# Scoring the two heads of a pair in the two row halves of TensorE, in a two-block transformer kernel

## The chip, the cores and the metric

One core of one Trainium2 chip runs the whole program. The metric is device time in microseconds (us), from the start of a launch to its end. The inputs are fp32, and the output is compared with the reference in fp32.

## The reference

Two transformer blocks on 512 tokens of width 1024. The first holds the change: its mixer is sparse attention of two kinds, and a mixture of 32 experts follows. The second block (differential attention and retention) is not touched.

```python
z = h @ w_in                                  # split into q, k, v of all branches
qn = rms_norm(q heads)                        # 8 NSA heads in 2 groups, 8 MoBA heads, 64 wide
kc = rms_norm(_compress(k_cmp)); vc = _compress(v_cmp)     # 31 compressed keys per group
s = qn . kc * scale - slope * distance;  p_cmp = masked_softmax(s);  o_cmp = p_cmp . vc
# selected branch and window branch: with 512 tokens both are causal attention over all keys
o_nsa = g0 * o_cmp + g1 * softmax(q . k_slc) . v_slc + g2 * softmax(q . k_win) . v_win
o_moba = softmax(q . k) . v                   # causal too at this length
x1 = x + gate * (concat(o_nsa, o_moba) @ w_out);  then the experts, then the second block
```

The scores need fp32 accuracy, so each factor is split into a high and a low part (fp32r, one pass of the array each), and products of parts are added in PSUM.

## The kernel before

The program is one list of instructions per engine, in the order in which Python generators yield. `first_half` computes the projections z in chunks (`zchunk`): a step is three matmuls of 512 columns (lines 257 to 259). `weave` runs such a main generator and, at a rate per step, one step of a background generator: compression (`compress`), the stacks of q (`q_stacks`), compressed scores (`compressed`), then `nsa`, which makes the stacks of k and calls `heads`.

`heads` works on 12 jobs. Jobs 0 to 7 are NSA (4 pairs of heads, 2 branches each), jobs 8 to 11 MoBA (4 pairs). A job is two heads, `hh` 0 and 1, and four tiles of 128 queries, `i` 3 to 0, against 512, 384, 256 and 128 keys (never under 256 columns on TensorE). In 8 rounds x, list A does the scores of the new job and list B the work of the job before: `turn` transposes the probabilities (line 917, copied out at 921 by ScalarE or VectorE), `pv` multiplies them by v (line 936, two heads in the two column halves of the array, 128*64). Each entry of A and B ends in a yield. A score tile is `scores` (lines 875 and 876), then on VectorE bias and maximum (line 881), on ScalarE the exponential (line 883). `normal` divides two tiles by their sum: reciprocal and gate on VectorE (894, 896), the products on GpSimd for head 0 (902) and on VectorE for head 1 (904).

To score a head of width 64 with all 128 rows, q is stacked: its high part lies in the head's own 64 rows, its low part in the other 64; k's high part stands twice, and so does its low part. Two passes then give all four products. `stacks` builds this from a transposed pair (`pair_turn`): a scaling to SBUF (334), copies (341, 343, 350) and subtractions (348, 351, 353), some of them moving data to the other half of the partitions. For MoBA this is done per job, in `prep`, while the job before is scored.

When the projections end, jobs 5 to 11 go on alone: `middle` loads `ada_w` in `mods` (lines 638 and 641, four column quarters), and takes 9 background steps between two of its loads, then drains the rest, and the output product follows (from 328.84 us). PSUM has a ring of three banks for scores and transposes while the projections run, and of six after. In the experts, line 1580 adds a bias by matmuls of 64 rows, in pairs: one in the upper and one in the lower half of the array's rows.

```python
    mm(ps[:, :w], lhsT=q, rhs=b.k[hh][0][:, :w], start=True, stop=False)     # 875
    mm(ps[:, :w], lhsT=q, rhs=b.k[hh][1][:, :w], start=False, stop=True)     # 876
```

Of the kernel before, what the change touches and what calls it, by code (L numbers as in the profile page):

```python
# [9 lines left out]
F32R = mybir.dt.float32r  # L10
# [4 lines left out]
OP = mybir.AluOpType  # L15
# [4 lines left out]
P = 128  # L20
# [167 lines left out]
class Build:  # L188
# [139 lines left out]
    def stacks(self, rows, c, gain, q=None, k=None, slow=False):  # L328
# [6 lines left out]
        if slow:  # L335
            yield
# [19 lines left out]
        yield  # L356

# [296 lines left out]
    def compress(self):  # L654
# [19 lines left out]

        self.kcb = ar.get(F32R)
# [74 lines left out]
        k0, k1 = kc[:, 0, :, 96:128], kc[:, 1, :, 96:128]  # L750
        nc.scalar.mul(k0, p2, gk)
        nc.vector.scalar_tensor_tensor(k1, p2, gk, k0, op0=OP.mult, op1=OP.subtract)
# [3 lines left out]
    def q_stacks(self):  # L756

        ar = self.ar
        self.qs = [ar.get(F32R), ar.get(F32R)]
        fb = ar.get()  # L760
        for c in range(4):
            self.f = fb.cols(c * T, T)
            yield from self.stacks(lambda i: self.qn.cols(i * T, T), c, self.gq[:, 0, c:c + 1],
                                   q=[self.qs[c // 2].cols((2 * (c % 2) + hh) * T, T) for hh in range(2)])
        ar.put(fb)
        ar.put(self.qn)

    def compressed(self):
# [10 lines left out]
        for g in range(2):  # L779
            ps = self.sb()  # L780
            for p in range(2):
                for j in range(4):
                    h = 4 * g + j
                    mm(ps, lhsT=self.kc[:, p, g, 96 - 32 * j:224 - 32 * j], rhs=self.qs[h // 4].cols((h % 4) * T, T),
                       start=(p == 0 and j == 0), stop=(p == 1 and j == 3))
# [75 lines left out]
    def heads(self, jobs):  # L861
# [6 lines left out]
        def scores(b, hh, i):  # L868
            n = (i + 1) * P
            w = max(n, 256)  # L870
            h = 2 * b.c + hh
            sl = 2.0 ** -(h % 8 + 1)
            ps = self.sb()
            q = b.q[hh][:, i * P:(i + 1) * P]
            mm(ps[:, :w], lhsT=q, rhs=b.k[hh][0][:, :w], start=True, stop=False)
            mm(ps[:, :w], lhsT=q, rhs=b.k[hh][1][:, :w], start=False, stop=True)
# [13 lines left out]
        def normal(b, hh, lo):  # L890
# [6 lines left out]
            for i in (lo + 1, lo):  # L897
# [49 lines left out]
        after = []  # L947
# [5 lines left out]
        for s in range(n + 1):  # L953
# [3 lines left out]
            if new:  # L957
                for hh in range(2):
                    for i in (3, 2, 1, 0):
                        A.append([lambda hh=hh, i=i: scores(new, hh, i)])  # L960
                        if i in (2, 0):
                            after.append(lambda new=new, hh=hh, i=i: normal(new, hh, i))
                            A[-1].append(len(after))
# [6 lines left out]
            for x in range(max(len(A), len(B))):  # L970
                if x < len(A):
                    A[x][0]()
                    yield
# [4 lines left out]
                if x % 2 == 0 and (x or old) and (A or not x):  # L978
                    after.pop(0)()
# [5 lines left out]
    def nsa(self):  # L985
# [4 lines left out]
        for c in range(4):  # L990
            for br in range(2):
# [4 lines left out]
                b.q = [self.qs[g].cols(((2 * c + hh) % 4) * T, T) for hh in range(2)]  # L996
                b.k = [self.kst[br, g]] * 2
# [8 lines left out]
    def moba(self):  # L1006
# [3 lines left out]
        for c in range(4):  # L1010
# [4 lines left out]
            def prep(b=b, c=c):  # L1015
                if c == 0:
                    self.flush()
                    mo.extend(ar.get(F32R) for _ in range(3))
# [3 lines left out]
                b.q = [mo[0].cols((2 * (c % 2) + hh) * T, T) for hh in range(2)]  # L1022
                b.k = [[mo[1 + c % 2].cols((2 * hh + x) * T, T) for x in range(2)] for hh in range(2)]
                self.f = self.cm.cols(512, T)
# [11 lines left out]
    def first_half(self):  # L1036
# [29 lines left out]
        self.bg = [self.compress(), self.q_stacks(), cmp]  # L1066
# [1365 lines left out]
```

## Time and profile before

| | |
|---|---|
| three runs | 1747.45, 1748.62, 1750.28 us (median 1748.62) |
| profiled execution | 1749.42 us, its span 1747.7 us |
| first scores of job 0, end of the projections | 139.35 us, 232.87 us |
| first scores of jobs 8, 9, 10, 11 | 267.7, 280.93, 294.87, 308.62 us |
| output product begins | 328.84 us |

A span is from the first to the last instruction; the 1.7 us around it are launch and end. A row of a timeline gives the start, the modelled length, the engine, the line and the operation, with output and inputs by name; 128*64 means that 128 rows and 64 columns of the array are used, 128x512 that 512 columns stream. Modelled ends of matmuls overlap the next start, so what a matmul costs is read from one start to the next. Releasers in brackets say who ended the idle time before.

### The profile page before, as it was taken

To read this page: it belongs to the slowest core of one execution; us is meant where nothing else is said; L and a number is where in the kernel's file an instruction comes from. 1 tells how busy PE (TensorE), PEld (TensorE's weight loads), DVE (VectorE), ACT (ScalarE), POOL (GpSimd) and SP (SyncE) were. 2 spreads that over 40 slices of the span, in tenths; PEclk is the share of its full clock that TensorE was granted. 3 is DMA by queue.
4 is the path that set the end of the run, shared out by engine and by line. 5 is a ranking of instruction groups with operands and counts; after the bars stand their busy time and mean duration, and the time that the engine had idled before them with its cause. 6 is when DMAs were issued, how large, how long until landed. Compare 5 with 4: busy or idle time off the path is not lost. (4 is left out here: it accounts for less than half of the span.)

```text
span 1747.7 us, 21964 instructions
## 1 busy us (share of the span) xinstructions
PE 1633.7 (93%) x7898; PEld 1046.9 (60%) x7899; DVE 1070.9 (61%) x1714; ACT 821.8 (47%) x1297; POOL 376.8 (22%) x259
## 2 busy tenths in 40 slices
PE   6999998897897999999999999999999989999998
PEld 4677755576742675565465464455455446778887
DVE  2567668668832475475485475476467486476653
ACT  4346568525521354254254255245245254477571
POOL 3012225222010120320321231231132130210120
PEclk9999999998999999999999999999999999999999
DMA  9812035467899999999999999999999986100301
GB/s 363 311 42 73 1 143 180 145 231 271 319 363 420 411 413 419 406 414 419 406 417 419 409 417 420 409 417 419 408 417 419 410 359 226 49 25 25 121 1 49
DMA packets 99975, 506.14 MB, mean 290 GB/s; under 512 B 10962, under 2 KB 20258, under 8 KB 48658
## 3 DMA queue, kind: packets, MB, share of 16 engines
q1 hardware_dynamic: 89972, 477.94, 67.1%
q0 software_dynamic: 9264, 25.68, 5.4%
q8 instruction: 64, 1.05, 0.2%
q10 hardware_dynamic: 624, 1.06, 0.2%
q14 instruction: 51, 0.42, 0.1%
HBM read 486.92 MB, written 17.71 MB: 289 GB/s over the span
## 5 line engine op out<-in xcount | busy, mean ns | idle before, releaser
L168 DVE TENSOR_TENSOR b<-b,b 128x1024 fp32r<-128x1024 f32 (+1 forms) x450 | 529.6, 1223 | 270.1 <-ACT b L167 269.4
L167 ACT CAST b<-b 128x1024 fp32r<-128x1024 f32 (+1 forms) x452 | 447.6, 1044 | 210.5 <-DMA b<-in_exp_w 168.7
L1737 POOL DMA_INDIRECT accd<-b,isc x15 | 154.9, 10325 | 405.3 <-DVE b L1732 388.5
L1590 PE MATMUL u<-b,b 128*64 128x512 f32 x1024 | 230.5, 597 | 0.3 <-DMA b<-in_exp_w 0.3
L257 PE MATMUL z<-b,b 128*128 128x512 f32 (+1 forms) x544 | 224.9, 414 | 2.9 <-ACT b L167 2.1
L258 PE MATMUL z<-b,b 128*128 128x512 f32 (+1 forms) x544 | 210.6, 387 | 1.5 <-DVE b L168 1.5
L257 PE MATMUL u<-b,b 128*96 128x512 f32 (+1 forms) x528 | 212.0, 401 | 0.0
L259 PE MATMUL z<-b,b 128*128 128x512 f32 (+1 forms) x544 | 210.6, 387 | 0.0
L259 PE MATMUL u<-b,b 128*96 128x512 f32 (+1 forms) x528 | 207.4, 393 | 0.0
L258 PE MATMUL u<-b,b 128*96 128x512 f32 (+1 forms) x528 | 207.4, 393 | 0.0
L1590 PEld LDWEIGHTS u<-b,b 128*64 128x64 f32 x1024 | 69.1, 136 | 129.2 <-issue 122.2
L257 PEld LDWEIGHTS z<-b,b 128*128 128x128 f32 x544 | 103.1, 190 | 33.4 <-issue 13.4
L258 PE MATMUL y<-b,b 128*96 128x512 f32 (+1 forms) x240 | 102.5, 427 | 18.5 <-DVE b L168 17.3
L1590 PE MATMUL y<-b,b 128*64 128x512 f32 x512 | 116.3, 605 | 0.8 <-DMA b<-in_exp_w 0.8
L259 PEld LDWEIGHTS z<-b,b 128*128 128x128 f32 x544 | 102.7, 189 | 21.9 <-DVE b L1929 0.4
L257 PE MATMUL y<-b,b 128*96 128x512 f32 (+1 forms) x240 | 100.6, 419 | 16.2 <-ACT b L167 16.2
L258 PEld LDWEIGHTS z<-b,b 128*128 128x128 f32 x544 | 103.3, 190 | 16.2 <-DVE b L168 2.5
L257 PEld LDWEIGHTS u<-b,b 128*96 128x96 f32 (+1 forms) x528 | 91.0, 172 | 35.2 <-ACT b L167 5.7
L259 PEld LDWEIGHTS u<-b,b 128*96 128x96 f32 (+1 forms) x528 | 90.8, 172 | 30.9
L258 PEld LDWEIGHTS u<-b,b 128*96 128x96 f32 (+1 forms) x528 | 90.9, 172 | 28.7 <-DVE b L168 0.2
L1609 ACT CAST b<-tr 128x768 fp32r<-128x768 f32 (+1 forms) x31 | 27.0, 871 | 157.8 <-PE tr L1607 155.3
L259 PE MATMUL y<-b,b 128*96 128x512 f32 (+1 forms) x240 | 98.8, 412 | 0.0
(516 smaller groups left out, 2098.5 us busy)
## 6 DMA issues: line engine op xcount, KB each, us to landing
b<-in_exp_w SPq DMA_DIRECT2D x384, 1024.0 KB, 20.8
b<-in_ada_w SPq DMA_DIRECT2D x24, 1024.0 KB, 5.7
b<-in_w_in SPq DMA_DIRECT2D x24, 1024.0 KB, 10.5
b<-in_w_out SPq DMA_DIRECT2D x8, 1024.0 KB, 4.9
b<-in_x SPq DMA_DIRECT2D x8, 512.0 KB, 7.3
b<-in_nsa_cmp_w POOLq DMA_DIRECT2D x2, 1024.0 KB, 8.8
b<-modd SPq DMA_DIRECT2D x4, 512.0 KB, 6.0
accd<-b SPq DMA_DIRECT2D x4, 512.0 KB, 4.5
```

What stands on the lines that cost most here:

```text
L167: nc.scalar.copy(hv, s)
L168: (other or nc.vector).tensor_tensor(out=lv, in0=s, in1=hv, op=OP.subtract)
L257: mm(out, lhsT=ah, rhs=bh, start=first, stop=False)
L258: mm(out, lhsT=ah, rhs=bl, start=False, stop=False)
L259: mm(out, lhsT=al, rhs=bh, start=False, stop=last)
L1590: mm(out[o, :], lhsT=lhsT, rhs=rhs[:, h * 512:(h + 1) * 512], start=False, stop=last, tile_position=(0, 64 * h), skip_group_check=True)
L1609: nc.scalar.copy(H[:, :, 0:n], pv)
L1737: nc.gpsimd.indirect_dma_start(out=self.accd, out_offset=bass.IndirectOffsetOnAxis(ap=self.isc[0:m, c:c + 1], axis=0), in_=ys[0:m, :], in_ ...
```

## The change

Each half of the rows now holds one head. `sides` makes a high part H (ScalarE, from PSUM) and a low part L (VectorE, from PSUM) of a transposed pair, and nothing moves to other partitions. `halves3` scores both heads of a pair in three passes, high by high, high by low, low by high (low by low is dropped), the two heads after each other in the two halves of the rows, into two PSUM banks. q of all heads and q and k of MoBA are made by `sides`; k of the NSA branches stays with `stacks`, which had it twice already. The compressed scores take three passes on two heads at a time, with the keys of a head in its own half (12 matmuls for 16). `heads` scores both heads at once in rounds 0, 2, 4 and 5, and normalizes in rounds 4 to 7, before the next job; before, one tile was scored per round, and the last normalization fell into the next job's round 0. Head 0's two short tiles move from GpSimd to VectorE. MoBA's stacks take two blocks of SBUF instead of three. The order of the DMAs on SyncE is the same in both.

```diff
+    def sides(self, rows, c, gain, H, L, apart=True):
+        ps = self.pair_turn(rows, c)
+        self.nc.scalar.mul(H, ps, gain)
+        if apart:
+            yield
+        self.nc.vector.scalar_tensor_tensor(L, ps, gain, H, op0=OP.mult, op1=OP.subtract)
...
+    def halves3(self, ps, q, k, qs, ks):
+        for x, y in ((0, 0), (0, 1), (1, 0)):
+            for hh in range(2):
+                s = slice(64 * hh, 64 * hh + 64)
+                self.nc.tensor.matmul(ps[hh], lhsT=q[x][s, qs], rhs=k[y][s, ks], start=(x + y == 0), stop=(x == 1))
...
-        def scores(b, hh, i):
+        def scores(b, i):
+            w = max((i + 1) * P, 256)
+            ps = [self.sb() for _ in range(2)]
+            self.halves3([p[:, :w] for p in ps], b.q, b.k, slice(i * P, (i + 1) * P), slice(0, w))
+            for hh in range(2):
+                least(b, hh, i, ps[hh])
...
-                if hh == 0:
+                if hh == 0 and lo:
                     nc.gpsimd.tensor_tensor(out=o, in0=o, in1=r[:, i - lo:i - lo + 1].to_broadcast([P, n]), op=OP.mult)
...
-                for hh in range(2):
-                    for i in (3, 2, 1, 0):
-                        A.append([lambda hh=hh, i=i: scores(new, hh, i)])
-                        if i in (2, 0):
-                            after.append(lambda new=new, hh=hh, i=i: normal(new, hh, i))
+                A = [lambda i=i: i is None or scores(new, i) for i in (3, None, 2, None, 1, 0, None, None)]
+                after = [lambda hh=hh, i=i: normal(new, hh, i) for i in (2, 0) for hh in range(2)]
...
-                if x % 2 == 0 and (x or old) and (A or not x):
-                    after.pop(0)()
+                if new and x >= 4:
+                    after[x - 4]()
...
-                yield from self.stacks(lambda i: self.km.cols(i * T, T), c, self.colb[:, 35:36], k=b.k, slow=True)
-                self.f = self.pb[2].cols(1280, T)
-                yield from self.stacks(lambda i: self.qm.cols(i * T, T), c, self.gq[:, 1, c:c + 1], q=b.q, slow=True)
+                yield from self.sides(lambda i: self.km.cols(i * T, T), c, self.colb[:, 35:36], *b.k)
+                yield from self.sides(lambda i: self.qm.cols(i * T, T), c, self.gq[:, 1, c:c + 1], *b.q)
```

Two places in the order of instructions. The first is TensorE while the projections run, in job 3 at the score tile of 384 keys; `z` are the banks of the projection, `a` those of scores and transposes. Before:

```order
L259 MATMUL z_1660<-b_137,b_154 128x512
L917 MATMUL a_1699<-ident,b_1106 128x128 x4
L257 MATMUL z_1657<-b_137,b_152 128x512
L258 MATMUL z_1657<-b_137,b_152 128x512
L259 MATMUL z_1657<-b_137,b_154 128x512
L875 MATMUL a_1713<-b_1115,b_1020 128x384
L876 MATMUL a_1713<-b_1115,b_1020 128x384
L257 MATMUL z_1658<-b_137,b_152 128x512
L258 MATMUL z_1658<-b_137,b_152 128x512
L259 MATMUL z_1658<-b_137,b_154 128x512
L917 MATMUL a_1721<-ident,b_1106 128x128 x4
```

With the change:

```order
L936 MATMUL a_1735<-ident,b_1093 128x128 x4
L257 MATMUL z_1674<-b_137,b_152 128x512
L258 MATMUL z_1674<-b_137,b_152 128x512
L259 MATMUL z_1674<-b_137,b_154 128x512
L372 MATMUL a_1744<-b_1102,b_1022 128x384
L372 MATMUL a_1745<-b_1102,b_1022 128x384
L372 MATMUL a_1744<-b_1102,b_1022 128x384
L372 MATMUL a_1745<-b_1102,b_1022 128x384
L372 MATMUL a_1744<-b_1102,b_1022 128x384
L372 MATMUL a_1745<-b_1102,b_1022 128x384
L257 MATMUL z_1675<-b_137,b_152 128x512
L258 MATMUL z_1675<-b_137,b_152 128x512
```

Two full-array matmuls for one head, between full-array matmuls, have become six half-row matmuls (line 372) for both heads; a projection step without any work of `heads` stands in front of some of them. In all, matmuls whose part of the array differs from that of the one before went from 26 to 66 between the start of the projection's chunk 3 and its end, and from 63 to 80 from there to the output product.

The second is VectorE where job 9 is scored after job 8, both MoBA. `ISA` with two outputs is the bias and maximum of a score tile, `mx` alone the reading of its accumulator. Before:

```order
L894 RECIPROCAL rs_2471<-rs_2471 128x2
L904 TENSOR_SCALAR b_1107<-b_1107,rs_2471 128x256
L904 TENSOR_SCALAR b_1107<-b_1107,rs_2471 128x128
L881 ISA b_1108,mx_2533<-z_2551,b_77 128x384
L881 ISA mx_2533 128x1
L921 COPY b_1109<-z_2555 128x512
L1199 TENSOR_SCALAR bf<-b_2403 128x128
L881 ISA b_1108,mx_2533<-a_2612,b_77 128x256
L881 ISA mx_2533 128x1
L894 RECIPROCAL rs_2532<-rs_2532 128x2
L351 TENSOR_TENSOR b_2260<-b_77,b_2260 64x512 x2
L353 TENSOR_TENSOR b_2260<-b_77,b_2260 64x512
```

With the change:

```order
L913 RECIPROCAL rs_2433<-rs_2433 128x2
L923 TENSOR_SCALAR b_1094<-b_1094,rs_2433 128x256
L923 TENSOR_SCALAR b_1094<-b_1094,rs_2433 128x128
L900 ISA b_1095,mx_2568<-a_2559,b_77 128x512
L900 ISA mx_2568 128x1
L900 ISA b_1094,mx_2571<-a_2560,b_77 128x512
L900 ISA mx_2571 128x1
L940 COPY b_1096<-z_2596 128x512
L362 SCALAR_TENSOR_TENSOR b_2309<-z_2590,colb,b_2309 128x512
L900 ISA b_1095,mx_2568<-a_2603,b_77 128x384
L900 ISA mx_2568 128x1
```

The last normalization of job 8 (head 1, its two short tiles) stood behind the first score tile of job 9 and now stands ahead of it. The three subtractions that made k's low part (351 twice, 353) are one operation from PSUM (362); that for q is likewise one for two (348).

## Rows read from the trace of the kernel before

**Rows 1.** the page: span, and busy time of each engine (share of span, instructions).
```profile
span 1747.7 us, 21964 instructions
PE 1633.7 (93%) x7898; PEld 1046.9 (60%) x7899; DVE 1070.9 (61%) x1714; ACT 821.8 (47%) x1297; POOL 376.8 (22%) x259
```

**Rows 2.** busy us of each engine by stretch; then PEclk, DMA share, GB/s.
```profile
139.30:232.90 93.60, 92.31 (x476) 67.36 (x476) 63.90 (x184) 54.45 (x136) 25.96 (x30) 1.00 0.10 34
232.90:280.90 48.00, 47.60 (x305) 25.79 (x303) 38.55 (x125) 35.02 (x93) 16.02 (x20) 1.00 0.47 176
280.90:294.90 14.00, 11.24 (x63) 6.72 (x61) 12.53 (x35) 11.53 (x29) 9.86 (x26) 1.00 0.64 195
294.90:308.60 13.70, 11.14 (x62) 6.67 (x60) 12.12 (x34) 11.20 (x28) 5.16 (x6) 1.00 0.72 274
308.60:328.80 20.20, 16.75 (x90) 9.68 (x88) 11.45 (x42) 10.27 (x30) 2.79 (x4) 0.92 0.00 1
```

**Rows 3.** timeline of PE between projection steps: start us, modelled us, instruction.
```profile
202.05 0.39 PE L259 MATMUL z<-b,b 128*128 128x512 f32 x1
202.28 0.28 PE L875 MATMUL a<-b,b 128*128 128x256 f32 x1
202.40 0.28 PE L876 MATMUL a<-b,b 128*128 128x256 f32 x1
...
206.72 0.33 PE L875 MATMUL a<-b,b 128*128 128x384 f32 x1
206.90 0.34 PE L876 MATMUL a<-b,b 128*128 128x384 f32 x1
```

**Rows 4.** timeline of PE in the experts, around a bias in row halves.
```profile
626.78 0.39 PE L259 MATMUL y<-b,b 128*128 128x512 f32 x1
627.09 0.73 PE L1580 MATMUL u<-b 64*128 64x512 f32 x4
627.75 0.50 PE L257 MATMUL u<-b,b 128*128 128x512 f32 x1
628.09 0.39 PE L258 MATMUL u<-b,b 128*128 128x512 f32 x1
```

**Rows 5.** timeline of PE, compressed scores of the first group.
```profile
125.94 0.63 PE L784 MATMUL a<-b,b 128*128 128x512 f32 x2
126.77 0.50 PE L784 MATMUL a<-b,b 128*128 128x512 f32 x1 [0.20 <-DVE b L348]
...
128.76 0.39 PE L257 MATMUL z<-b,b 128*128 128x512 f32 x1
```

**Rows 6.** what PE waited for, 280.9 to 328.8 us: total, times, longest.
```profile
PE a L917 <- DVE b L904: 3.3, 2, 1.9
PE z L917 <- DVE b L904: 2.9, 2, 1.5
PE a L936 <- DVE b L921: 1.0, 2, 0.5
```

**Rows 7.** groups of DVE, 280.9 to 308.6 us (count, then busy us and mean ns).
```profile
L351 DVE TENSOR_TENSOR b<-b,b 64x512 fp32r<-64x512 f32 x4 | 5.4, 1342 | 0.7 <-ACT b L343 0.6
L348 DVE TENSOR_TENSOR b<-b,b 64x512 fp32r<-64x512 f32 x4 | 2.7, 686 | 1.2 <-ACT b L341 1.1
L353 DVE TENSOR_TENSOR b<-b,b 64x512 fp32r<-64x512 f32 x2 | 2.0, 1004 | 0.0
...
L904 DVE TENSOR_SCALAR b<-b,rs 128x256 f32<-128x256 f32 x2 | 0.7, 356 | 0.1
L904 DVE TENSOR_SCALAR b<-b,rs 128x128 f32<-128x128 f32 x2 | 0.6, 276 | 0.0
```

**Rows 8.** group of DVE, whole span: a low part made from PSUM.
```profile
L2028 DVE SCALAR_TENSOR_TENSOR b<-a,colb,b 128x512 fp32r<-128x512 f32 x4 | 2.8, 744 | 3.2 <-ACT b L2027 3.2
```

**Rows 9.** timeline of PE in job 9, two of its waits.
```profile
284.94 0.66 PE L917 MATMUL a<-ident,b 128*128 128x128 f32 x4 [1.37 <-DVE b L904]
...
292.85 1.08 PE L936 MATMUL a<-b,b 128*64 128x384 f32 x6 [0.50 <-DVE b L921]
```

More of the change, by code (lines that the diff above doesn't have):

```diff
@@ L326, in pair_turn, with stacks @@
         return ps
-    def stacks(self, rows, c, gain, q=None, k=None, slow=False):
+    def stacks(self, rows, c, gain, q=None, k=None):
         nc = self.nc
@@ L356, in stacks @@
         yield
+    def sides(self, rows, c, gain, H, L, apart=True):
[4 more added lines that the diff above has]
+        self.nc.vector.scalar_tensor_tensor(L, ps, gain, H, op0=OP.mult, op1=OP.subtract)
+        if not apart:
+            yield
+        yield
+    def halves3(self, ps, q, k, qs, ks):
[3 more added lines that the diff above has]
+                self.nc.tensor.matmul(ps[hh], lhsT=q[x][s, qs], rhs=k[y][s, ks], start=(x + y == 0), stop=(x == 1))
     def rms_over(self, v, n, tag, scale, then):
@@ L749, in compress, with q_sides, q_pair @@
         p2 = ps[:, 0:64].rearrange("p (g n) -> p g n", g=2)
-        k0, k1 = kc[:, 0, :, 96:128], kc[:, 1, :, 96:128]
-        nc.scalar.mul(k0, p2, gk)
-        nc.vector.scalar_tensor_tensor(k1, p2, gk, k0, op0=OP.mult, op1=OP.subtract)
+        for hh in range(2):
+            s, o = slice(64 * hh, 64 * hh + 64), 96 + 32 * hh
+            k0, k1 = kc[s, 0, :, o:o + 32], kc[s, 1, :, o:o + 32]
+            nc.scalar.mul(k0, p2[s], gk[s, :])
+            nc.vector.scalar_tensor_tensor(k1, p2[s], gk[s, :], k0, op0=OP.mult, op1=OP.subtract)
         yield
         ar.put(kkb, ktb)
-    def q_stacks(self):
+    def q_sides(self):
         ar = self.ar
         self.qs = [ar.get(F32R), ar.get(F32R)]
-        fb = ar.get()
         for c in range(4):
[L762 to L765, printed above, removed]
+            yield from self.sides(lambda i: self.qn.cols(i * T, T), c, self.gq[:, 0, c:c + 1], *self.q_pair(c))
         ar.put(self.qn)
+    def q_pair(self, c):
+        return [self.qs[c // 2].cols((2 * (c % 2) + x) * T, T) for x in range(2)]
     def compressed(self):
@@ L780, in compressed @@
             ps = self.sb()
[L781 to L785, printed above, removed]
+            for x, y in ((0, 0), (0, 1), (1, 0)):
+                for j in range(0, 4, 2):
+                    mm(ps, lhsT=self.kc[:, x, g, 96 - 32 * j:224 - 32 * j], rhs=self.q_pair(2 * g + j // 2)[y],
+                       start=(x + y + j == 0), stop=(x == 1 and j == 2))
             t = wb.cols(1280, T)
@@ L866, in heads, with least @@
         pend = []
-        def scores(b, hh, i):
+        def scores(b, i):
+            w = max((i + 1) * P, 256)
+            ps = [self.sb() for _ in range(2)]
+            self.halves3([p[:, :w] for p in ps], b.q, b.k, slice(i * P, (i + 1) * P), slice(0, w))
+            for hh in range(2):
+                least(b, hh, i, ps[hh])
+        def least(b, hh, i, ps):
             n = (i + 1) * P
-            w = max(n, 256)
             h = 2 * b.c + hh
             sl = 2.0 ** -(h % 8 + 1)
[L873 to L876, printed above, removed]
             if i == NT - 1:
@@ L946, in heads @@
         n = len(jobs)
-        after = []
         for s, b in enumerate(jobs):
@@ L971, in heads @@
                 if x < len(A):
-                    A[x][0]()
+                    A[x]()
                     yield
@@ L995, in nsa @@
                 g = c // 2
-                b.q = [self.qs[g].cols(((2 * c + hh) % 4) * T, T) for hh in range(2)]
-                b.k = [self.kst[br, g]] * 2
+                b.q, b.k = self.q_pair(c), self.kst[br, g]
                 v = lambda j, br=br, g=g: self.vv.cols(br * 512 + j * P + g * 64, 64)
@@ L1017, in prep @@
                     self.flush()
-                    mo.extend(ar.get(F32R) for _ in range(3))
+                    mo.extend(ar.get(F32R) for _ in range(2))
                 elif c == 1:
@@ L1021, in prep @@
                     self.early = [ar.get() for _ in range(5)]
-                b.q = [mo[0].cols((2 * (c % 2) + hh) * T, T) for hh in range(2)]
-                b.k = [[mo[1 + c % 2].cols((2 * hh + x) * T, T) for x in range(2)] for hh in range(2)]
-                self.f = self.cm.cols(512, T)
-                yield from self.stacks(lambda i: self.km.cols(i * T, T), c, self.colb[:, 35:36], k=b.k, slow=True)
-                self.f = self.pb[2].cols(1280, T)
-                yield from self.stacks(lambda i: self.qm.cols(i * T, T), c, self.gq[:, 1, c:c + 1], q=b.q, slow=True)
+                b.q, b.k = [[mo[c % 2].cols((2 * o + x) * T, T) for x in range(2)] for o in range(2)]
+                yield from self.sides(lambda i: self.km.cols(i * T, T), c, self.colb[:, 35:36], *b.k)
+                yield from self.sides(lambda i: self.qm.cols(i * T, T), c, self.gq[:, 1, c:c + 1], *b.q)
                 if c == 3:
```

5 lines of the change are left out of this document (1 added, 4 removed).

## The prediction

> **What bounds the kernel now.** I read the page's busy shares first: TensorE is busy for 93% of the span, VectorE for 61% [rows 1]. A mean over stages says little, so the next view is busy time by stretch [rows 2], cut at first scores of jobs: job 0 to the end of the projections, jobs 5 to 8 with the loads of `ada_w` between them, job 9, job 10, then job 11 with what follows until the output product. In the first two TensorE is busy for 92.31 of 93.60 us and 47.60 of 48.00: there its work is the time, and a microsecond added to it is a microsecond of the kernel. In jobs 9 and 10 it is busy for 11.24 of 14.00 and 11.14 of 13.70, while VectorE has 12.53 and 12.12: there VectorE, and the chain through it, sets the pace. The list of TensorE's waits says the same: it waits for the normalization of head 1 (line 904) before a transpose, 3.3 and 2.9 us, and for a copy (line 921) before `pv` [rows 6]; in job 9 these are 1.37 and 0.50 us [rows 9]. So the change has two accounts: TensorE's work from 139 to 281 us, and VectorE's and the waits from 281 to 329 us.
>
> **Score passes.** Among projection steps a 512-column matmul takes 0.23 us from start to start (202.05 to 202.28), one of 256 columns 0.12, one of 384 columns 0.18 [rows 3]. One pass over a job's four tiles is 0.23 + 0.18 + 0.12 + 0.12 = 0.65 us. A pair of heads took four passes (two heads, two each), and takes three if two half-row matmuls run side by side. That they do is seen in the experts: four half-row matmuls of 512 columns (line 1580) are followed by the next full one 0.66 us after their start, 627.09 to 627.75 [rows 4]; one after the other they would need 4 x 0.23 = 0.92. So 0.65 us are saved per job: 5 x 0.65 = 3.25 us in jobs 0 to 4, 7 x 0.65 = 4.55 in jobs 5 to 11. The compressed scores go from 16 to 12 matmuls of 512: 4 x 0.23 = 0.92 us.
>
> **Switches of the array's shape.** This is the cost that the diff doesn't show. From the last full matmul before the line-1580 group (626.78) to the second full one after it (628.09) are 1.31 us [rows 4]. They hold four streams of 512 columns, the full one, two half-row pairs and the full one, or 4 x 0.23 = 0.92. The other 0.39 us is two switches, 0.195 each: the next shape starts only once the array is empty, and its first weights are loaded with nothing beside them. A score tile after a projection step, both in full shape, pays nothing of the kind (202.05, 202.28, 202.40) [rows 3]. By the count of the order, 40 switches are added while the projections run and 17 after. At 0.195 that is +7.8 us and +3.3 us. The ends of this unknown are about nothing a switch, as in rows 3, and the 0.195 of rows 4, where the group also waits for results of its own engine; I take 0.195, since those are the same half-row shapes.
>
> The Trainium skill, TensorEngine Tiling (Array Packing), section Key Properties, states that changing the tiling mode drains TensorE. By that rule the score groups, which now stand alone between full-array work, pay twice each; without it the sum below would be 11.1 us lower. The trace agrees, with the 0.39 us [rows 4].
>
> **First part.** +7.8 - 3.25 - 0.92 = +3.6 us. Against it: the first group of compressed scores waits for the stacks of q, which ScalarE and VectorE make piece by piece; its 8 matmuls take from 125.94 to 128.76, 2.82 us for 8 x 0.23 = 1.84 of work, and a releaser named is the subtraction of line 348 [rows 5]. `sides` drops two copies on ScalarE and one of two VectorE operations per pair, so I let the 0.98 us go. Net **+2.65 us**. TensorE's queue holds the projection behind each score group, so nothing covers it.
>
> **VectorE in jobs 9 and 10.** Lines 351, 348 and 353 go: 5.4 + 2.7 + 2.0 = 10.1 us in the two jobs [rows 7]. In come four operations of line 362, two per job; the nearest row is another low part made from PSUM at the same size, 744 ns [rows 8], so 2.98 us. Head 0's short tiles come over from GpSimd, at head 1's price 356 + 276 ns [rows 7] per job, 1.26 us. Net -5.9 us on 27.70, from busy 24.65 [rows 2]. TensorE is busy there for 22.38, which its passes and switches (-0.65 + 17/7 x 0.195 = -0.18 a job) leave at 22.0, so the two jobs can't fall below that; some wait stays between them, and I take **-5.0**. Its ends are 0 and -5.7. The five copies per job that leave ScalarE (busy for 11.53 of 14.00) and the two that leave GpSimd [rows 2] bring nothing of their own.
>
> **Job 11 and the tail.** 20.20 us with 16.75 busy on TensorE [rows 2]. The longest wait, 1.9 us for line 904 [rows 6], was for the last normalization of the job before, which now precedes the new job's scores. I take **-2.0**, with ends 0 and -3.45.
>
> **A new wait.** Between the transposes of round 5 and `pv` of round 6 TensorE had scores to do, and still waited 0.50 us in job 9 [rows 9]. Outside the projections nothing stands there now. Queued on VectorE ahead of that copy are two maxima instead of one; behind it stand the normalizations, whose reciprocal waits for the last exponential, and then the next job's maxima. I add 0.4 us in jobs 5 to 7, **+1.2**, ends 0 and 3.0; in jobs 9 to 11 it is within the sums above. Job 8 keeps its time: TensorE has the loads' matmuls to do.
>
> **Sum.** First part +2.65; passes and switches of jobs 5 to 11, -4.55 + 3.3 = -1.25; jobs 9 and 10 -5.0; job 11 -2.0; new wait +1.2: **-4.4 us**. The profiled execution took 1749.42, so 1745.0. It lies 0.8 us above the median of the three runs, 1748.62; in terms of that median I forecast **1744.2 us**. What a measurement of this kernel can tell from no change is 0.2%, 3.5 us.
>
> **Rivals.**
> - *No relief after the projections.* The waits move instead of going: transposes of head 0 now follow their own normalization by two rounds, where it was four, and ScalarE's last exponential sits in between. Then jobs 9 to 11 keep their pace, and 7 us of the sum are lost: 1751.2. For it speaks that each job's normalizations now come in four rounds in a row; against it that VectorE loses 5.9 us of work in two jobs, and that its chain (two maxima, a copy, four products) is about as long as what TensorE does meanwhile (two `pv` and a score group).
> - *Slower: banks.* While the projections run there are three PSUM banks, and a score group takes two at once. A following group or transpose may have to wait until the first maximum has left its bank. If 20 groups wait for 0.5 us each, 10 us are added: 1754. It decides if VectorE is more than about two projection steps (2 x 3 x 0.23 = 1.4 us) behind. Against it: VectorE is busy for 63.90 of 93.60 us there [rows 2]. The Trainium skill has a sentence on this in TensorEngine Tiling (Array Packing), Gotcha 1: row tiles write to different PSUM banks, which raises the pressure on them. No run here shows what it costs.
> - *Switches cost nothing*, for instance since weights are loaded ahead: 1744.2 - 11.1 = 1733. Rows 4 speak against it.
> - *The halves don't overlap.* Then a pair needs six passes: 12 x 3 x 0.65 = 23.4 us more, 1767.6. Rows 4 speak against it, with weights and operands laid out in the same way.
>
> **How the numbers follow.** Forecast 0.52 (with its own ends of the sums, 1739 to 1749); no relief 0.25; banks 0.12; switches free 0.08; no overlap 0.03. Faster by over 0.2% means under 1745.1: of the forecast's 0.52 some 0.42, all of 0.08, and a little of the second, where half the relief is lost: 0.52 in all. Slower means over 1752.1: the banks and no overlap, 0.15, and a part of "no relief" with a longer new wait, 0.05: 0.20. The same is 0.28. The range 1737 to 1754 leaves out the free switches below, and above the missing overlap and the worse half of the banks.
>
> **What would show it.** In the profile of the changed kernel: half-row score matmuls starting in pairs; about 0.4 us more than the streams around each score group; the stretch from job 0's scores to the projections' end longer than 93.6 us by 3 to 5 us; jobs 9 and 10 at 10.8 to 11.8 us each; the waits for line 904 (now 923) gone from the transposes of head 1. I am wrong if the first stretch does not grow, or if jobs 9 and 10 stay near 13.7 us.

## The result and the profile after

The changed kernel took **1760.09 us** (median of four runs, 1759.92 to 1761.32) beside 1749.45 for the one before (four runs too). The ratio on record is 1.0077, 95% interval 1.0063 to 1.0090; the two medians alone give 1.0061, and against the 1747.1 to 1747.9 us that the kernel before took beside the later runs it would be 1.0070 to 1.0074. By each of these it is slower, by 11 to 13 us, where 4.4 us less were forecast, and it lies above the range (up to 1754). The profiled execution has a span of 1758.3 us, 10.6 more than [rows 1]:

```profile
span 1758.3 us, 22073 instructions
PE 1633.6 (93%) x7990; PEld 1037.7 (59%) x7991; DVE 1064.1 (61%) x1723; ACT 803.6 (46%) x1270; POOL 354.6 (20%) x227
```

TensorE's total of busy time, 1633.6 us for 1633.7 before, tells nothing about the 10.6 us: it grew by 6.4 us in the first of the stretches below and fell in others, by 2.8 us even behind the first expert, where both kernels run the same program for the same time. Where the 10.6 us lie is seen by stretches, cut at the same places as [rows 2]: job 0's scores to the projections' end, jobs 5 to 8, job 9, job 10, job 11 and the tail, and then the output product and the router up to the first expert (busy us of PE, PEld, DVE, ACT, POOL; PEclk, DMA share, GB/s):

```profile
138.40:239.60 101.20, 98.70 (x515) 64.08 (x514) 67.86 (x194) 54.06 (x138) 19.61 (x20) 0.98 0.09 32
239.60:287.60 48.00, 46.39 (x331) 23.67 (x330) 35.04 (x133) 28.73 (x84) 7.30 (x8) 1.00 0.42 154
287.60:305.40 17.80, 12.32 (x77) 6.85 (x76) 9.30 (x32) 8.59 (x24) 6.59 (x22) 0.90 0.47 143
305.40:318.00 12.60, 10.29 (x71) 6.25 (x70) 9.57 (x34) 8.11 (x23) 1.82 (x2) 1.00 1.03 408
318.00:335.60 17.60, 15.60 (x97) 8.88 (x96) 11.06 (x41) 9.06 (x26) 1.82 (x2) 1.00 0.14 53
335.60:423.00 87.40, 71.26 (x420) 57.24 (x419) 58.90 (x138) 27.08 (x59) 27.41 (x28) 0.92 0.57 219
```

The last of these stretches in the kernel before:

```profile
328.80:412.50 83.70, 71.06 (x421) 56.95 (x420) 57.55 (x136) 26.87 (x59) 26.96 (x28) 0.92 0.65 242
```

Four differences make the 10.6 us: job 0 starts 0.9 earlier (138.43 for 139.35); from there to the projections' end are 101.2 for 93.5 (+7.7); jobs 5 to 11 take 96.0 as before, since job 9 lost 3.8 and jobs 10 and 11 gained 1.1 and 2.6; product and router take 87.4 for 83.7 (+3.7). Behind the first expert both need 1335 us.

**The projections.** One score group of 512 keys in TensorE's timeline:

```profile
138.11 0.39 PE L259 MATMUL z<-b,b 128*128 128x512 f32 x1
138.43 0.96 PE L372 MATMUL a<-b,b 64*128 64x512 f32 x6
139.32 0.50 PE L257 MATMUL z<-b,b 128*128 128x512 f32 x1
139.66 0.40 PE L258 MATMUL z<-b,b 128*128 128x512 f32 x1
```

From 138.11 to 139.66 are 1.55 us. They hold five streams of 0.23 (one full, three pairs of halves, one full), 1.15; 0.40 remain, 0.20 a switch, as in [rows 4]. Two halves do run side by side. What TensorE waited for in this stretch:

```profile
PE a L372 <- DVE mx L900: 1.4, 1, 1.4
PE a L936 <- DVE mx L900: 1.1, 2, 0.8
```

In the kernel before:

```profile
PE z L257 <- ACT b L567: 0.5, 1, 0.5
PE a L875 <- DVE mx L881: 0.4, 1, 0.4
PE a L819 <- DVE mx L881: 0.4, 1, 0.4
```

The waits with the change are for a bank whose maximum VectorE has not yet taken, 2.5 us; before, such waits took 0.8 us of 1.3. But idle time is the smaller part: of the 7.7 us that the stretch grew by, 6.4 us are busy time of TensorE (98.70 for 92.31). The mean granted clock is 0.98, where it was 1.00 [rows 2].

**Job 9.** Its timeline on TensorE has one large hole, and SyncE's own waits name the cause: the issue of an `ada_w` load waited 22.5 us for `pv` (line 955).

```profile
287.58 0.97 PE L372 MATMUL a<-b 64*128 64x512 f32 x6
292.61 1.94 PE L657 MATMUL z<-b,b 128*32 128x512 f32 x8 [4.07 <-DMA b<-in_ada_w]
```

```profile
SPq L643 <- PE a L955: 22.5, 1, 22.5
```

**The rest of the waits from 239.6 to 335.6 us**, beside [rows 6]:

```profile
PE z L657 <- DMA b<-in_ada_w: 4.1, 1, 4.1
PE z L936 <- DVE b L362: 2.3, 3, 1.2
PE a L936 <- DVE b L362: 1.6, 2, 1.3
PE z L936 <- DVE b L923: 1.2, 1, 1.2
...
PE a L936 <- DVE b L923: 0.4, 2, 0.2
```

The normalization (923, before 904) holds TensorE for 1.6 us instead of 6.2. New are 3.9 us for line 362: a transpose wants the bank from which `sides` still makes its low part.

**Product and router.** VectorE, GpSimd and TensorE around the largest hole:

```profile
347.88 3.38 DVE L1551 TENSOR_SCALAR b<-pidf 128x128 fp32r<-128x128 f32 x1
351.17 0.68 DVE L1216 TENSOR_TENSOR b<-z,b 128x512 f32<-128x512 f32 x1
351.89 3.32 DVE L1217 TENSOR_TENSOR b<-b,b 128x512 f32<-128x512 f32 x1
```

```profile
347.27 7.38 POOL L1542 TENSOR_TENSOR b<-b,b 32x1536 fp32r<-32x1536 f32 x2 [21.20 <-ACT b L1540]
```

```profile
349.29 0.39 PE L259 MATMUL z<-b,b 128*128 128x512 f32 x1
355.31 1.08 PE L1285 MATMUL a<-ident,b 128*128 128x128 f32 x4 [5.64 <-issue]
...
356.62 0.63 PE L258 MATMUL z<-b,b 128*128 128x512 f32 x1
357.05 0.63 PE L259 MATMUL z<-b,b 128*128 128x512 f32 x1
```

GpSimd subtracts the experts' biases in two operations, 347.27 to 354.65. Two operations of VectorE on SBUF alone (lines 1551 and 1217) take 3.38 and 3.32 us; the one between them, of the same size as line 1217 but with an input in PSUM (1216), takes its 0.68. The trace names no releaser for the transpose, but it starts 0.1 us after line 1217 has ended (355.21). TensorE then runs at the lower of its two clocks, 1.2 GHz: 0.43 us from one start to the next (356.62 to 357.05) instead of 0.23.

### The profile page after: what moved, and what is told of

The parts are those of the page before. It is cut to its first block, busy times and chain, and to the rows that moved or that the text cites. A ratio compares the mean times of both kernels' runs of the same rounds, so it can differ in the third digit from the quotient of the medians.

```text
span 1758.3 us, 22073 instructions
## 1 busy us (share of the span) xinstructions
PE 1633.6 (93%) x7990; PEld 1037.7 (59%) x7991; DVE 1064.1 (61%) x1723; ACT 803.6 (46%) x1270; POOL 354.6 (20%) x227
## 5 line engine op out<-in xcount | busy, mean ns | idle before, releaser
L258 PE MATMUL y<-b,b 128*96 128x512 f32 (+1 forms) x240 | 101.2, 422 | 19.1 <-DVE b L168 18.0
L257 PE MATMUL y<-b,b 128*96 128x512 f32 (+1 forms) x240 | 98.9, 412 | 18.9 <-ACT b L167 18.9
L259 PE MATMUL y<-b,b 128*96 128x512 f32 (+1 forms) x240 | 97.1, 405 | 0.0
```

The costliest lines, as they stand in the source:

```text
L257: mm(out, lhsT=ah, rhs=bh, start=first, stop=False)
L258: mm(out, lhsT=ah, rhs=bl, start=False, stop=False)
L259: mm(out, lhsT=al, rhs=bh, start=False, stop=last)
```

## The experiments

My theory after the result had three parts. (1) The late load of `ada_w` comes from the blocks of SBUF: with two blocks for MoBA's stacks instead of three, the blocks go round in another order, and the last load gets the block of v of the NSA branches, which job 7's `pv` still reads. (2) The hole in the product's stage is GpSimd holding VectorE, at a phase that the same rotation shifted. (3) The projections pay for the switches and for the two banks that a group takes. The rivals: VectorE's chain would have held job 9 anyway; the halves, or the order, did all of it.

All stretches in us, from the profiled executions; "first" is from job 0's scores to job 5's, "second" from there to the output product, "third" to the first expert, "rest" to the end. Where kernels run the same program in a stretch, its time repeats within 0.6 us in the first two, and within 2.6 us in the rest, the four kernels with halves for MoBA only left aside.

| kernel | ratio to before, 95% interval | first | second | third | rest |
|---|---|---|---|---|---|
| before | 1 | 93.5 | 96.0 | 83.7 | 1335.1 |
| after | 1.0077 (1.0063 to 1.0090) | 101.2 | 96.0 | 87.4 | 1335.2 |
| three_blocks | 1.0011 (1.0000 to 1.0022) | 101.2 | 90.6 | 81.4 | 1334.9 |
| vv_early | 1.0040 (1.0027 to 1.0053) | 101.2 | 90.7 | 87.1 | 1335.4 |
| bias_later | 1.0053 (1.0038 to 1.0067) | 101.2 | 96.2 | 84.8 | 1336.3 |
| bias_dve | 1.0057 (1.0043 to 1.0070) | 100.7 | 95.9 | 84.4 | 1334.7 |
| pieces | 1.0045 (1.0029 to 1.0062) | 100.7 | 95.7 | 80.5 | 1335.3 |
| order_alone | 1.0029 (1.0017 to 1.0041) | 97.7 | 93.7 | 83.3 | 1337.3 |
| moba_halves | 1.0017 (1.0007 to 1.0027) | 97.7 | 90.1 | 86.0 | 1338.8 |
| small_together | 1.0008 (0.9999 to 1.0017) | 100.1 | 90.3 | 81.2 | 1334.7 |
| mix | 1.0004 (0.9992 to 1.0015) | 93.5 | 89.7 | 86.7 | 1336.8 |
| mix_small_pieces | 1.0001 (0.9989 to 1.0013) | 93.5 | 89.7 | 82.6 | 1339.5 |
| mix_pieces | 0.9988 (0.9977 to 0.9999) | 93.6 | 89.7 | 84.1 | 1338.8 |
| before_pieces | 1.0003 (0.9994 to 1.0012) | 93.5 | 95.5 | 84.1 | 1335.1 |

Beside these runs the kernel before took 1747.11 to 1747.89 us (medians of 17 to 23 runs, single ones from 1743.71 to 1752.72). Its profiled execution of 1749.42 us was thus some 2 us longer than its usual one, so ratios and stretches are compared, not times of single runs.

### Three blocks again

```diff
-                    mo.extend(ar.get(F32R) for _ in range(2))
+                    mo.extend(ar.get(F32R) for _ in range(3))
```

> The changed kernel, but MoBA's stacks take three blocks of SBUF again (the third stays empty), so that the blocks go round as they did before. Theory: the 4.07 us that TensorE waits for the last load of ada_w in job 9 come from the block that this load got, the one of v of the NSA branches, which job 7's products still read. Then the last load is issued some 10 us earlier than at 287.68, the wait goes, and job 9 (17.85 us) falls to 13.0 to 13.9; the stretch of half clock that follows the wait at 292.5 goes too. The output product begins at 330 to 331.6 instead of 335.62, and the whole takes 1754 to 1756, if the stage of the product and the router stays at 87.4 us. Rival: VectorE's chain would have held job 9 anyway; then the product still begins after 334 and the whole takes 1758.5 to 1760.

Windows of jobs 5 to 8, 9, 10, 11 and the tail, and the third stretch:

```profile
239.70:287.70 48.00, 46.38 (x331) 23.70 (x330) 35.06 (x133) 28.72 (x84) 7.29 (x8) 1.00 0.47 176
287.70:300.20 12.50, 10.80 (x79) 6.20 (x78) 9.28 (x32) 8.66 (x24) 6.59 (x22) 1.00 0.40 99
300.20:312.70 12.50, 10.20 (x70) 6.17 (x70) 9.46 (x32) 8.11 (x23) 1.82 (x2) 1.00 1.02 398
312.70:330.40 17.70, 15.69 (x98) 8.97 (x97) 11.11 (x41) 9.06 (x26) 1.82 (x2) 1.00 0.05 17
330.40:411.70 81.30, 69.15 (x420) 55.59 (x419) 56.76 (x136) 27.19 (x59) 27.41 (x28) 0.96 0.67 249
```

Job 9 falls from 17.8 to 12.5 us: the 4.07 us of waiting, and the lower clock behind it (0.90 before, 1.00 now). Part (1) is shown. The product begins at 330.36. The third stretch falls too, by 6.0 us, which I had not put into the number: the whole took 1749.8 us, less than the 1754 to 1756 expected. By the two ratios one allocation accounts for 0.66% of the 0.77%.

### The block of v to the rows of x

```diff
+                    t = ar.get()
                     self.early = [ar.get() for _ in range(5)]
+                    ar.put(t)
```

> The changed kernel, with two blocks for MoBA's stacks, but the block of v of the NSA branches goes to the rows of x (among the five that middle uses later) and another, long free, to the last load of ada_w. Theory: the same 4.07 us go as in the run with three blocks, the product begins at 330 to 331.6, and the whole takes 1754 to 1756. It differs from the run with three blocks in the blocks that the loads of w_out get later: here the third should stay early (before 315 us), with three blocks it should come late, as before the change (332). If the late third load was what kept the product's first steps and GpSimd's subtraction apart, then the stage of the product and the router is shorter with three blocks (near 83.7) than here (near 87.4). Rival: as for three blocks, 1758.5 to 1760.

The second stretch is 90.7 us, as with three blocks (90.6): only the late load's block counts there. The third stays at 87.1. SyncE's issues of the three loads of `w_out` (first start, time from there to the last issue's end) with three blocks, and then here:

```profile
305.21 29.09 SPq L135 DMA_DIRECT2D b<-in_w_out  x3
```

```profile
299.43 5.29 SPq L135 DMA_DIRECT2D b<-in_w_out  x3
```

With three blocks the third load waits until 334 us for its block, as before the change; here, as in the changed kernel, all are out before the product begins. Then the product's first steps run ahead, and GpSimd's subtractions meet other operations of VectorE: 81.4 or 87.1 us. Here they meet the same two as in the changed kernel (3.39 and 3.32 us), and TensorE's wait at the transpose is back:

```profile
PE a L1287 <- issue: 5.6, 1, 5.6
```

With three blocks line 1217 takes 0.99 us beside them, an operation of one column (line 1257) is held instead (2.58 us), and TensorE waits 0.2 us at that place. That the phase decides is shown by this pair; by what mechanism, by the next three runs.

### GpSimd's subtractions: later, on VectorE, in pieces

```diff
-        split()
         self.weave(main, limit=4)
+        split()
```

> The changed kernel with the splitting of the experts' biases (a cast on ScalarE, two subtractions on GpSimd of 3.69 us each, a selection on VectorE) four steps of the product later. Theory: VectorE's operations of 3.38 us (line 1551, 128x128) and 3.32 us (line 1217) each end within 0.6 us of a subtraction on GpSimd and are held by it, and TensorE's 5.64 us of waiting at the transpose of line 1285 follow from that. With the subtractions elsewhere, the operation of line 1217 takes 0.69 us again, that wait falls under 2 us, and the stage of the product and the router takes 83 to 85 us instead of 87.43: 1755.5 to 1757.5 in all. Rival: the wait has another cause (the loads of the biases, the order of the steps); then the stage stays within 1 us of 87.4.

The third stretch is 84.8. The operation of line 1217 that had been held takes 0.69 us, but the next one of that line meets the first subtraction and takes 3.33, and the tiny one of line 1257 meets the second (2.56). The collision was moved, not removed. The stage came out as expected, the whole (1758.5 us) 1 us above.

```diff
-                nc.gpsimd.tensor_tensor(out=b[o:o + 32, :n], in0=f[o:o + 32, :n], in1=b[o:o + 32, :n], op=OP.subtract)
+                nc.vector.tensor_tensor(out=b[o:o + 32, :n], in0=f[o:o + 32, :n], in1=b[o:o + 32, :n], op=OP.subtract)
```

> The changed kernel with the two subtractions of the experts' biases on VectorE instead of GpSimd, at the same place. Theory (GpSimd holds VectorE): without GpSimd beside it, the operations of lines 1551 and 1217 take 0.22 and 0.69 us again; the subtractions cost VectorE two operations of 1536 columns, about 2.1 us each (three times the 0.69 us of 512 columns in line 1217). So VectorE loses 4.2 us where it lost 5.8 us (3.38 + 3.32 - 0.22 - 0.69): the wait of 5.64 us falls by 1 to 2 us only, and the whole takes 1758 to 1759. Rival: VectorE was slow there for itself, not because of GpSimd; then the operations of lines 1551 and 1217 stay at 3.3 us and the whole takes 1763 or more.

VectorE's timeline:

```profile
347.58 3.52 DVE L1542 TENSOR_TENSOR b<-b,b 32x1536 fp32r<-32x1536 f32 x2
351.11 0.23 DVE L1551 TENSOR_SCALAR b<-pidf 128x128 fp32r<-128x128 f32 x1
351.25 0.69 DVE L1216 TENSOR_TENSOR b<-z,b 128x512 f32<-128x512 f32 x1
351.97 0.69 DVE L1217 TENSOR_TENSOR b<-b,b 128x512 f32<-128x512 f32 x1
```

Without GpSimd's subtractions both operations have their short times, so it was GpSimd. The subtractions cost 3.52 us, not the 4.2 I had put, and TensorE's hole fell to 3.5 us.

```diff
-                nc.gpsimd.tensor_tensor(out=b[o:o + 32, :n], in0=f[o:o + 32, :n], in1=b[o:o + 32, :n], op=OP.subtract)
+                for s in range(0, n, 512):
+                    nc.gpsimd.tensor_tensor(out=b[o:o + 32, s:s + 512], in0=f[o:o + 32, s:s + 512], in1=b[o:o + 32, s:s + 512],
+                                            op=OP.subtract)
```

> The changed kernel, with each of the two subtractions on GpSimd (32x1536) in three pieces of 512 columns. Theory: GpSimd keeps VectorE's operation waiting until its own one ends, so a piece of 3.69 / 3 = 1.23 us holds it for 1.3 us at most: the operations of lines 1551 and 1217 take under 1.5 and 2.0 us instead of 3.38 and 3.32, TensorE's wait of 5.64 us falls to 2.5 to 3.5, and the stage of the product and the router to 84 to 85.5 us from 87.4: 1756.5 to 1758.5 in all (ratio 1.0050 to 1.0062). Rival: VectorE gets no turn between two operations of GpSimd that follow each other; then both stay above 3 us and the ratio stays near 1.0077.

```profile
348.80 1.21 DVE L1553 TENSOR_SCALAR b<-pidf 128x128 fp32r<-128x128 f32 x1
349.93 0.68 DVE L1216 TENSOR_TENSOR b<-z,b 128x512 f32<-128x512 f32 x1
350.64 1.07 DVE L1217 TENSOR_TENSOR b<-b,b 128x512 f32<-128x512 f32 x1
```

Held for at most one piece: 1.21 and 1.07 us. The hole at the transpose fell from 5.64 to 1.2 us, and the stretch by 6.9 to 80.5, twice what I had put; the mean granted clock in it is 0.96 for 0.92, so the lower clock behind the hole went with it. The Trainium skill, SBUF — State Buffer, section SBUF: two separate sides, has this rule: a VectorE operation in a two-port mode, or one with two inputs in SBUF beside a GpSimd operation that reads SBUF, and the GpSimd operation exclude each other for a whole instruction. The trace agrees for line 1217, with two inputs in SBUF, and for line 1216, whose one input lies in PSUM and which is not held (0.68 us); which mode line 1551 ran in is not in the trace.

### The order alone

The kernel before, with both heads scored in a round and the normalizations in rounds 4 to 7.

```diff
+            ps = [self.sb() for _ in range(2)]
+            for hh in range(2):
+                q = b.q[hh][:, i * P:(i + 1) * P]
+                for x in range(2):
+                    mm(ps[hh][:, :w], lhsT=q, rhs=b.k[hh][x][:, :w], start=(x == 0), stop=(x == 1))
...
```

> The kernel before with the order of the changed one, and nothing else: both heads' tiles scored in one round (four full-shape matmuls into two banks, 0, 2, 4, 5), normalizations in rounds 4 to 7, head 0's short tiles on VectorE. Stacks, passes, shapes and blocks of SBUF are as before. Theory (order is harmless, the halves cost the first stretch): from job 0's scores to the projections' end 94.0 to 95.5 us, against 93.5 before and 101.2 after, the waits for two banks in it; from there to the output product 92 to 95 us against 95.97, as the 6.2 us of waits for the last normalization go and VectorE keeps its load; 1744.5 to 1749.5 in all. Rival: the order is what made the projections longer, by the two banks that a score group takes; then the first stretch takes 98 us or more, and the whole 1751 or more.

The first stretch takes 97.7 us, between theory (95.5) and rival (98 or more); the whole, 1752.5 us, is on the rival's side. What TensorE waited for in the first stretch:

```profile
PE a L874 <- DVE mx L886: 2.3, 2, 1.6
PE a L922 <- DVE mx L886: 1.3, 2, 0.8
PE a L922 <- DVE b L909: 0.6, 1, 0.6
PE a L819 <- DVE mx L886: 0.4, 1, 0.4
```

These are 4.6 us, against 1.3 in the kernel before, in full shape and with no switch added: 3.3 of the 4.2 us are waits, nearly all for VectorE's maxima, that is for banks. The halves add 3.5 us on top (101.2). The second stretch gains 2.3 us from the order.

### Halves for MoBA only

```diff
+            if b.gate is None:
+                self.halves3([p[:, :w] for p in ps], b.q, b.k, slice(i * P, (i + 1) * P), slice(0, w))
+            for hh in range(2 if b.gate else 0):
...
+                yield from self.sides(lambda i: self.km.cols(i * T, T), c, self.colb[:, 35:36], *b.k)
+                yield from self.sides(lambda i: self.qm.cols(i * T, T), c, self.gq[:, 1, c:c + 1], *b.q)
```

> The run with the order alone, and the halves for MoBA only (jobs 8 to 11: stacks by the new helper, three passes in row halves); the NSA jobs score in full rows, four passes; three blocks for MoBA's stacks. Theory: no switch of shape is added while the projections run, so the first stretch is that of the order alone, 94 to 95.5 us; VectorE loses 10.1 - 3.0 us of work in jobs 9 and 10, and the stretch from the projections' end to the product falls to 89.5 to 92 us (90.7 with halves everywhere and three blocks). In all 2 to 4 us less than the order alone: 1741 to 1746. Rival: what the halves give after the projections they give in the NSA jobs 5 to 7; then this stretch stays above 93 us, and the whole is within 1 us of the order alone.

First stretch 97.7, as with the order alone, and second 90.1, as the theory had it: `sides` and the halves together are worth 3.6 us for MoBA (no run has one without the other, so VectorE's relief alone is not measured), and the halves in the NSA jobs give nothing there (90.6 with them). The third stretch (86.0, GpSimd again) and the rest (1338.8) took back most of it: 1749.9 us in all, above the 1741 to 1746 expected.

### The short tiles in one group

```diff
-                A = [lambda i=i: i is None or scores(new, i) for i in (3, None, 2, None, 1, 0, None, None)]
+                A = [lambda t=t: t and scores(new, *t) for t in ((3,), (), (2,), (), (1, 0), (), (), ())]
...
```

> The changed kernel with three blocks, and the tiles of 256 and 128 keys of a job scored in one group: twelve half-row matmuls of 256 columns in the two halves of two banks. The streams are the same; by the order 10 of 63 changes of shape go while the projections run, and 7 of 79 after. Theory (a change of shape costs 0.195 us of TensorE): the first stretch falls by 10 x 0.195 = 1.95 us from 101.2 to 99.2, and the second by up to 1.4 us: 2 to 3.4 us less than with three blocks (ratio to before 0.9985 to 1.0003). Rival: the two banks that are held through four maxima make transposes wait longer, and eat it up; then the first stretch stays at 101 or above, and waits for maxima in it exceed 2.6 us.

The first stretch fell by 1.1 us, the second by 0.3. Ten switches less were to give 1.95; the waits for maxima grew from 2.6 to 3.3 us. Both the price of a switch and the rival's waits are seen in it. The ratio, 1.0008 for 1.0011 with three blocks, is not told apart from that one, and lies above the 0.9985 to 1.0003 expected.

### The change for MoBA alone

The NSA jobs as before, with their order; MoBA with helper, halves and new order; three blocks.

```diff
+            pair = new and new.gate is None
+            if pair:
+                A = [[lambda i=i: i is None or both(new, i)] for i in (3, None, 2, None, 1, 0, None, None)]
+                own = [lambda hh=hh, i=i: normal(new, hh, i) for i in (2, 0) for hh in range(2)]
+            elif new:
...
```

> The kernel before with the change for MoBA alone: jobs 8 to 11 get their stacks by the new helper, score in row halves, both heads in a round, and normalize in rounds 4 to 7; three blocks. The NSA jobs, their order included, stay as before. Theory: the change's gain lies after the projections, its price in them. Then the first stretch is that of before, 93.5 us (97.7 with the new order, 101.2 with the halves too); the jobs 5 to 7 take the 34.8 us they took, and 8 to 11 with the rest up to the product 55.5 to 56.5 us, as in the run with halves for MoBA (271.0 to 326.8): the product begins at 323 to 324.5 instead of 328.84. With a stage of product and router of 81 to 87 us, by how GpSimd's subtractions fall, 1740 to 1747 in all, ratio 0.995 to 0.999. Rival: the order in the NSA jobs 5 to 7 is what the gain needs; then the product begins at 327 or later, and the ratio is 1.000 or more.

```profile
139.00:232.50 93.50, 92.29 (x475) 67.38 (x475) 63.76 (x184) 54.45 (x136) 25.96 (x30) 1.00 0.11 35
232.50:322.20 89.70, 83.24 (x545) 46.26 (x543) 63.45 (x229) 55.40 (x159) 20.54 (x40) 1.00 0.46 167
322.20:408.90 86.70, 71.52 (x422) 57.15 (x421) 56.00 (x138) 27.20 (x59) 27.31 (x28) 0.92 0.62 234
```

Up to the product it is as expected: 93.5, and 89.7 for 96.0. But the ratio is 1.0004: the third stretch took 86.7 (VectorE's line 1241 was held for 3.43 us), and the rest 1.7 us more than before. Two runs with the subtractions in pieces followed, one of them with MoBA's short tiles in one group.

> The run with the change for MoBA alone, and in it MoBA's two short tiles in one group, and GpSimd's subtractions in pieces of 512 columns. Theory: four groups fewer stand between full-shape work, at most 8 x 0.195 = 1.6 us, of which waits keep a part: the product begins up to 1 us earlier than with MoBA alone. The stage of the product and the router takes 80 to 83 us whatever the phase, since no operation of VectorE is held for over 1.4 us. In all 1738 to 1743, ratio 0.9945 to 0.9975. Rival: the pieces cost GpSimd and VectorE more than they give (the stage stays above 83.5 us); then it is no faster than the run with MoBA alone.

> The run with the change for MoBA alone, with GpSimd's subtractions in pieces of 512 columns, and MoBA's short tiles in groups of their own as in the change. Theory: the product begins at 322 to 323 us, as with MoBA alone; its stage falls from 86.66 to 81 to 83 us, since the operation of VectorE that was held for 3.43 us is held for 1.3 at most. In all 3 to 5 us less than MoBA alone: 1742.5 to 1745, ratio 0.9965 to 0.9990. Rival: what is won up to the first expert is lost again behind it, as in the run with MoBA, small tiles and pieces, where the rest took 1339.45 us against 1335.13; then the ratio is 0.999 to 1.001 and the rest over 1338 us.

The pieces brought the third stretch to 82.6 and 84.1 (80 to 83 and 81 to 83 expected). The short tiles in one group gave nothing: the second stretch is 89.7 in both, and their ratio is 1.0001 for 0.9945 to 0.9975 expected. In the rest both lost some 4 us, as the second run's rival had it. Most of that falls into one place, a block of the experts behind a branch, here in mix_pieces (TensorE's timeline):

```profile
1435.68 0.47 PE L257 MATMUL u<-b,b 128*96 128x512 f32 x1
1438.47 0.40 PE L258 MATMUL u<-b,b 128*96 128x512 f32 x1 [2.32 <-issue]
1438.70 0.48 PE L259 MATMUL u<-b,b 128*96 128x512 f32 x1
1438.98 0.63 PE L257 MATMUL u<-b,b 128*96 128x512 f32 x1
```

TensorE stands for 2.32 us between two matmuls of one step, with no releaser, and then runs at the lower clock (0.63 modelled). The twelve matmuls from 1435.68 on take 6.9 us, for 2.85 in the kernel before: 4.1 us more, where its rest lost 3.6. The three other kernels with halves for MoBA only stand for 1.5 to 2.1 us there (the same twelve take 6.8, 4.5 and 5.2 us in moba_halves, mix and mix_small_pieces); the kernel before, the changed one and all the others show none. The cause is open and was not tried. Still mix_pieces, at 0.9988 (0.9977 to 0.9999), has the lowest ratio of all, and the only interval below 1; it is less than the 0.2% that I took for a difference that can be told, and one such interval among thirteen can be chance.

> The kernel before with GpSimd's two subtractions in pieces of 512 columns, and nothing else. There the second addition of line 1207 was held for 0.7 us and the tiny operation of line 1247 for 2.4 us. Theory: both waits fall to 1.2 us or less, and the stage of the product and the router from 83.66 us to 81 to 83; ratio 0.998 to 1.000. Rival: in that phase nothing on the path hangs on them; the stage stays at 83.5 us or more and the ratio at 1.000.

Here the rival was right (third stretch 84.1, ratio 1.0003): in the phase of the kernel before little hangs on what GpSimd holds. So the pieces mend a collision; they are no gain of their own.

## Why the prediction was wrong

- **The step that failed is one that the sum did not have.** "MoBA's stacks take two blocks of SBUF instead of three" stands in the description of the change, and the prediction gives it no term. It cost 5.3 us in job 9 (late load, lower clock) and 6.0 us in the product's stage, by the collision with GpSimd that it set up. That the DMAs keep their order on SyncE said nothing about the block, and so the wait, of each. Between the forecast of -4.4 and the +10.6 us of the profiled executions lie 15.0 us, and three blocks take back 11.3 of them. With three blocks the ratio is 1.0011, which by the 0.2% of the prediction is no change: the forecast of a faster kernel fails even then, by two terms that were sized wrong, the first stretch and jobs 9 and 10.
- **Passes: right.** Pairs of halves run side by side, three streams a group.
- **Switches: right in price** (0.40 us a group for 0.39 forecast). The rivals "switches cost nothing" and "halves don't overlap" fall. The Trainium skill, TensorEngine Tiling (Array Packing), section Key Properties, says that a change of tiling mode drains TensorE; the trace agrees, with these 0.40 us, and the rule spoke against the change.
- **The first stretch came out 3 us too long**, +7.7 for +4.55 (7.8 - 3.25). The rival on banks has its part: the new order alone costs 4.2 us there, 3.3 of it waits. I priced it at 20 waits of 0.5 us with a chance of 0.12, as an alternative to the forecast; it came beside it, in a few waits of up to 1.6 us. In the changed kernel itself the waits are 2.5 us, 1.2 more than before. The lower clock (0.98) is worth 0.5 us: in bias_dve and pieces, the same program up to the product, the granted clock of this stretch is 1.00 and it takes 100.7 us. Some 1.4 us stay open.
- **First compressed scores:** -0.9 us for -1.9. A transpose now waits 1.9 us for line 362, the same wait for a low part that shows up after the projections; how much of the missing 1.0 us is its doing was not tried.
- **Jobs 5 to 11: right in kind, too large.** Forecast -7.05 (-1.25 - 5.0 - 2.0 + 1.2); with three blocks -5.3. Job 11 with the tail gave 2.5 for 2.0. Jobs 9 and 10 gave 2.7 for 5.0, at 12.5 us each instead of 10.8 to 11.8. VectorE's busy time in them fell by 5.9 us as forecast (from 24.65 to 18.74), but the time did not follow it: the waits for the normalization went from 6.2 to 1.6 us, as foreseen, but 4.2 us of waits for line 362 came (over jobs 5 to 11). I had taken `sides` as VectorE's saving and not asked who stands behind its bank. Jobs 5 to 8 kept their 48.0.
- **"No relief after the projections"** had the right time for this stretch (0 us), for the wrong reason: the relief was there, and the load ate it.
- **Product and router** were taken as untouched. They come after the last changed line, but their loads and their phase hang on blocks and times set before.

## What to carry to other kernels

A buffer more or less in a rotating pool is an edit with a price of its own: list for each later transfer which buffer it now gets, who read that buffer last, and when. A switch of the array's shape, 0.2 us here, has to be weighed against the pass that it saves: among projection steps the halves cost 3.5 us, in jobs 5 to 7 they gave nothing, and for MoBA they won 3.6 us together with the shorter making of the stacks. A stage that follows a change should be read for operations of VectorE that run beside long ones of GpSimd, since a shift of a few us can make or break a collision there. Where one profile stands for a kernel, compare stretches, and leave room for a difference of some 2 us that comes from the execution and not from the program.

## What was not expected of the hardware

- GpSimd's 3.7 us operation made a VectorE operation of 0.23 us take 3.38; six pieces made it 1.21 (in the changed kernel, bias_dve and pieces).
- Two stalls of TensorE were paid twice: after 4.07 and after 5.64 us of waiting it ran at 1.2 GHz for a while (mean granted clock 0.90 in job 9; behind the second, matmuls 0.43 us apart instead of 0.23). In job 9 without the wait (three_blocks) the clock was 1.00.
- TensorE can stand for over 2 us between two matmuls of a step with nothing in the trace that it waits for (2.32 us, between 1435.68 and 1438.47 in mix_pieces).
